# Other places in SBUF for the tile pools of a two-layer encoder kernel

## The chip, the cores and the metric

The kernel runs on one core of one Trainium2 chip. The metric is device time in microseconds of one execution of the whole program: the median of three runs before the change is 2350.79 us (2350.09 to 2352.40). The profile is of one more execution, which took 2351.57 us; from its first to its last instruction it spans 2349.8 us.

## The reference

Two encoder layers on one sequence of 512 tokens, width 1024, in float32, then a final RMSNorm. Cut to what matters:

```python
for l in range(2):
    xn = rmsnorm(x, norm1_g[l])
    h = xn @ w_in[l]                                  # split into the inputs of four mixers
    ys = [gdn_mixer, diff_mixer, swa_mixer, mlstm_mixer]   # each (512 tokens, 512 wide)
    branch = einsum('bsnw,nwd->bsnd', stack(ys), w_branch[l])
    gate = sigmoid(einsum('bsd,dne->bsne', xn, w_gate[l]))
    x = x + sum(gate * branch, axis=2) @ w_out[l]
    xn = rmsnorm(x, norm2_g[l])
    x = x + square(relu(xn @ w_mlp1[l])) @ w_mlp2[l]
return rmsnorm(x, final_norm_g)
```

## The kernel before, in words

Every dense product is computed with operands split into two parts, a high one of type float32r and a low one that holds what is left (`xh` and `xl`, `wh` and `wl`, `hh` and `hl`, `mh` and `ml`), as three matmuls that add up in one PSUM bank: high by high, high by low, low by high. A stream of dense work (projections, gates, merges, MLP) fills the time between the steps of the four mixers, which are written as generators; in the MLP, from the output projection on, the dense stream is alone.

There are three forms of dense work, and the text calls them by their lines.

- L392 to L394 (`run_a`): the activations are the stationary operand (128x128, loaded by LDWEIGHTS) and the weights, 256 columns, move. It does the input projections that are wanted token by token (stationary `xh`, `xl`), the output projection `wo` (stationary `mh`, `ml`) and the second MLP product `m2` (stationary `hh`, `hl`). Line 718 to 720 do the last slice of `m2` in the same order of matmuls, with weights kept in `twh` and `twl`.
- L406 to L408 (`run_b`) and L435 to L437 (`run_b2`): the weights are stationary and 512 columns of activations move.
- L832 to L834: the first MLP product `m1`, a fast scheme of seven products for two by two blocks; weights stationary, 256 columns of activations (`xh`, `xl`, or sums of them, `xsh`, `xsl`) move.

The order of the three matmuls in `run_a`, for one 128-token block `tt` and one 128-row slice `k4`:

```python
th, tl = xh[kt][:, blk(tt)], xl[kt][:, blk(tt)]
mm(o, th, wh[:, k4, :], start=(kt == 0 and tt % 2 == 0), stop=False)     # L392
mm(o, th, wl[:, k4, :], start=False, stop=False)                         # L393
mm(o, tl, wh[:, k4, :], start=False, stop=(kt == kts - 1 and tt % 2 == 1))   # L394
```

Tiles come from six pools in SBUF. A pool takes a stretch of every partition when it is opened, and the stretches follow each other in the order of the lines that open the pools.

```python
def A(dt=F32, s="t", w=S):              # pool ar: 26 buffers
    return ar.tile([P, 516], dt, tag="ar", name=nm(s))[:, :w]
def B(dt=F32, s="b", w=2048):           # pool bg: 13 buffers
    return bg.tile([P, 2080], dt, tag="bg", name=nm(s))[:, :w]
```

`bg` holds the large activation tiles, 2080 values or 8320 bytes a partition: `x`, `xh`, `xl`, `hh`, `hl`, `mh`, `ml`, `twh`, `twl`, the raw weights `wq` of `m1`, and what the mixers keep. `wp` holds the weights of the other dense work, 4096 bytes a partition: two buffers of raw weights (`wr`, filled by DMA), three of `wh`, three of `wl`. `ar` holds 26 tiles of 2064 bytes, placed 2080 apart, for everything of 512 columns, `xsh` and `xsl` among it. `sp` holds columns of a few values, `cp` the constants, `lp` what one layer keeps. A pool hands its buffers out in turn as they come free, so `hh` and `hl` stand in other `bg` buffers each time.

The bytes of a partition that each pool has, in the program before and in the changed one (the first 16512 bytes are taken by other things in both):

| pool | before | changed |
|---|---|---|
| cp | 16512 to 27424 | 211520 to 222432 |
| lp | 27424 to 31392 | 222432 to 226400 |
| wp | 31392 to 64160 | 124672 to 157440 |
| sp | 64160 to 66720 | 226400 to 228960 |
| ar | 66720 to 120800 | 157440 to 211520 |
| bg | 120800 to 228960 | 16512 to 124672 |

Buffer number i of `bg` begins at 120800 + 8320 i before and at 16512 + 8320 i in the changed program. Inside the tiles, the slices that `run_a` reads begin at multiples of 512 bytes.

Of the kernel before, what the change touches and what calls it, by code (L numbers as in the profile page):

```python
# [30 lines left out]
NAR = 26  # L31
NBG = 13
# [81 lines left out]
def encoder(ctx: ExitStack, tc: tile.TileContext, a: dict, out: bass.AP, dbg: dict = None):  # L114
    nc = tc.nc
    dbg = dbg or {}
    pe, dve, act, pool = nc.tensor, nc.vector, nc.scalar, nc.gpsimd
    mm = pe.matmul
    cp = ctx.enter_context(tc.tile_pool(name="cp", bufs=1))
    lp = ctx.enter_context(tc.tile_pool(name="lp", bufs=1))  # L120
    wp = ctx.enter_context(tc.tile_pool(name="wp", bufs=3))
    sp = ctx.enter_context(tc.tile_pool(name="sp", bufs=8))
    ar = ctx.enter_context(tc.tile_pool(name="ar", bufs=NAR))
    bg = ctx.enter_context(tc.tile_pool(name="bg", bufs=NBG))
    dr = ctx.enter_context(tc.tile_pool(name="dr", bufs=1, space=bass.MemoryType.DRAM))
    pd = ctx.enter_context(tc.tile_pool(name="pd", bufs=4, space=bass.MemoryType.PSUM))
    pm = ctx.enter_context(tc.tile_pool(name="pm", bufs=4, space=bass.MemoryType.PSUM))
# [1623 lines left out]
```

## Time and profile before

| | |
|---|---|
| median of three runs | 2350.79 us |
| profiled execution | 2351.57 us |
| its span, first to last instruction | 2349.8 us |
| PE (TensorE matmul) busy | 2285.3 us, 97% |
| PEld (weight load) busy | 2083.2 us, 89% |
| DVE, ACT, POOL busy | 1582.2, 1187.5, 747.6 us |
| mean granted TensorE clock | 0.996 of full speed |
| DMA | 200.72 MB, the hardware queue's packets fill 27.5% of 16 engines' time |

PE is what is busy nearly always. Its matmuls are pipelined: one takes some 280 ns from start to end, while the next starts after less than half of that. So the time that a matmul costs is read from start to start: a stretch of time divided by the matmuls that it starts.

### The profile page before, as it was taken

The page shows a single profiled execution, that of the slowest core. Times are in us where ns is not written, and L with a number is a line of the kernel's source. Part 1 is how long each engine was busy: PE and PEld are TensorE (multiplying, and loading weights), DVE is VectorE, ACT ScalarE, POOL GpSimd, SP SyncE. Part 2 cuts the span into 40 slices and gives each one's busy share as a digit, 9 for nine tenths or more (in the row PEclk, how much of TensorE's full clock was granted, in tenths as well). Part 3 has the DMA queues.
Part 4 walks back from the last instruction along what each step waited for, and adds up shares of the span by engine and source line. Part 5 has one row for each costly group of instructions (what it writes and reads, how often), then busy time and mean ns, then how long its engine had stood idle before and what let it go on. Part 6 is the DMA issues. An engine that isn't in the chain of part 4 may idle for free. (4 is left out here: it accounts for less than half of the span.)

```text
span 2349.8 us, 43335 instructions
## 1 busy us (share of the span) xinstructions
PE 2285.3 (97%) x16992; PEld 2083.2 (89%) x16992; DVE 1582.2 (67%) x2988; ACT 1187.5 (51%) x2777; POOL 747.6 (32%) x806
## 2 busy tenths in 40 slices
PE   7999999999999999999999999999999999999998
PEld 6879987989888989999987799879898889899998
DVE  5774547685786477677767745587767854867775
ACT  4565444654665264344445654365546643534443
POOL 1135552132232134343200555412313310434341
PEclk9999999999999999999999999999999999999999
DMA  6322131222122523333323112321221234233322
GB/s 149 99 46 64 55 95 57 60 88 80 51 71 74 160 71 122 95 109 108 111 74 90 55 55 64 91 63 52 93 82 55 72 106 131 90 97 109 99 82 90
DMA packets 234779, 200.72 MB, mean 85 GB/s; under 512 B 31696, under 2 KB 223824, under 8 KB 234576
## 3 DMA queue, kind: packets, MB, share of 16 engines
q1 hardware_dynamic: 231408, 192.75, 27.5%
q10 hardware_dynamic: 2304, 4.20, 0.5%
q8 instruction: 133, 2.18, 0.4%
q0 software_dynamic: 864, 1.02, 0.2%
q14 instruction: 70, 0.57, 0.1%
HBM read 190.04 MB, written 8.39 MB: 84 GB/s over the span
## 5 line engine op out<-in xcount | busy, mean ns | idle before, releaser
L293 DVE TENSOR_TENSOR wl<-wr,wh 128x512 fp32r<-128x512 f32 x540 | 400.4, 762 | 183.4 <-ACT wh L292 176.1
L292 ACT CAST wh<-wr 128x512 fp32r<-128x512 f32 x540 | 317.0, 621 | 219.0 <-PE pd L436 59.2
L392 PE MATMUL pd<-wh,xh 128*128 128x256 f32 x960 | 279.4, 291 | 0.0
L393 PE MATMUL pd<-wl,xh 128*128 128x256 f32 x960 | 269.8, 281 | 0.0
L394 PE MATMUL pd<-wh,xl 128*128 128x256 f32 x960 | 269.4, 281 | 0.0
L394 PE MATMUL pd<-wh,hl 128*128 128x256 f32 x896 | 248.2, 277 | 0.0
L392 PE MATMUL pd<-wh,hh 128*128 128x256 f32 x896 | 248.0, 277 | 0.0
L393 PE MATMUL pd<-wl,hh 128*128 128x256 f32 x896 | 248.0, 277 | 0.0
L292 ACT CAST wh<-wq 128x512 fp32r<-128x512 f32 x196 | 115.3, 619 | 220.4 <-PE pd L394 94.0
L435 PE MATMUL pd<-xh,wh 128*128 128x512 f32 (+1 forms) x544 | 217.7, 401 | 0.5 <-ACT xh L222 0.5
L436 PE MATMUL pd<-xl,wh 128*128 128x512 f32 (+1 forms) x544 | 209.0, 384 | 1.8 <-DVE xl L223 1.6
L437 PE MATMUL pd<-xh,wl 128*128 128x512 f32 (+1 forms) x544 | 208.8, 384 | 0.0
L293 DVE TENSOR_TENSOR wl<-wq,wh 128x512 fp32r<-128x512 f32 x196 | 181.9, 962 | 13.4 <-ACT wh L292 13.3
L393 PEld LDWEIGHTS pd<-wl,xh 128*128 128x128 f32 x960 | 181.9, 189 | 1.4
L392 PEld LDWEIGHTS pd<-wh,xh 128*128 128x128 f32 x960 | 181.5, 189 | 1.4
L394 PEld LDWEIGHTS pd<-wh,xl 128*128 128x128 f32 x960 | 181.3, 189 | 0.2
L809 POOL TENSOR_TENSOR wq<-wq,wq 128x512 f32<-128x512 f32 x84 | 124.4, 1488 | 163.1 <-DVE wl L293 153.7
L393 PEld LDWEIGHTS pd<-wl,hh 128*128 128x128 f32 x896 | 168.2, 188 | 0.0
L394 PEld LDWEIGHTS pd<-wh,hl 128*128 128x128 f32 x896 | 168.2, 188 | 0.0
L392 PEld LDWEIGHTS pd<-wh,hh 128*128 128x128 f32 x896 | 168.1, 188 | 0.0
L677 DVE TENSOR_TENSOR x<-pd,x 128x512 f32<-128x512 f32 x124 | 85.1, 689 | 101.4 <-PE pd L394 101.4
L1011 POOL TENSOR_TENSOR r<-r,r 128x512 f32<-128x512 f32 (+1 forms) x28 | 35.5, 1266 | 325.8 <-DVE r L1010 185.9
(394 smaller groups left out, 6656.9 us busy)
## 6 DMA issues: line engine op xcount, KB each, us to landing
wr<-in_w_in SPq DMA_DIRECT2D x92, 512.0 KB
wr<-in_w_mlp SPq DMA_DIRECT2D x72, 512.0 KB
wr<-in_w_gate SPq DMA_DIRECT2D x64, 512.0 KB
wq<-in_w_mlp SPq DMA_DIRECT2D x56, 512.0 KB
wr<-in_w_branch SPq DMA_DIRECT2D x32, 512.0 KB
wr<-in_w_out SPq DMA_DIRECT2D x16, 512.0 KB
x<-in_x SPq DMA_DIRECT2D x16, 256.0 KB
gsd<-gs ACTq DMA_DIRECT2D x16, 256.0 KB
```

What stands on the lines that cost most here:

```text
L292: act.copy(wh[:, k:k + n], raw[:, k:k + n])
L293: dve.tensor_tensor(wl[:, k:k + n], raw[:, k:k + n], f(wh[:, k:k + n]), op=ALU.subtract)
L392: mm(o, th, wh[:, k4, :], start=(kt == 0 and tt % 2 == 0), stop=False)
L393: mm(o, th, wl[:, k4, :], start=False, stop=False)
L394: mm(o, tl, wh[:, k4, :], start=False, stop=(kt == kts - 1 and tt % 2 == 1))
L435: mm(o, w1_, xh[kt][:, sl], start=(kt == 0 and hi_ == 0), stop=False)
L436: mm(o, w1_, xl[kt][:, sl], start=False, stop=False)
L437: mm(o, w2_, xh[kt][:, sl], start=False, stop=last)
L677: dve.tensor_tensor(d, bank.rearrange("p (t c) -> p t c", t=2), d, op=ALU.add)
L809: pool.tensor_tensor(d[:, k:k + 2], x[:, k:k + 2], y[:, k:k + 2], op=op)
L1011: pool.tensor_tensor(v(t1), v(t1), v(t2), op=ALU.add)
```

## The change

The lines that open the pools are put in another order: `bg`, `wp`, `ar`, `cp`, `lp`, `sp` in place of `cp`, `lp`, `wp`, `sp`, `ar`, `bg`. Sizes, counts of buffers, tags and all instructions stay. On every engine the instructions of the two programs stand in the same order, row for row, with the same waits and the same buffer numbers; only the byte addresses of the operands in SBUF differ.

```diff
     mm = pe.matmul
+    bg = ctx.enter_context(tc.tile_pool(name="bg", bufs=NBG))
+    wp = ctx.enter_context(tc.tile_pool(name="wp", bufs=3))
+    ar = ctx.enter_context(tc.tile_pool(name="ar", bufs=NAR))
     cp = ctx.enter_context(tc.tile_pool(name="cp", bufs=1))
     lp = ctx.enter_context(tc.tile_pool(name="lp", bufs=1))
-    wp = ctx.enter_context(tc.tile_pool(name="wp", bufs=3))
     sp = ctx.enter_context(tc.tile_pool(name="sp", bufs=8))
-    ar = ctx.enter_context(tc.tile_pool(name="ar", bufs=NAR))
-    bg = ctx.enter_context(tc.tile_pool(name="bg", bufs=NBG))
     dr = ctx.enter_context(tc.tile_pool(name="dr", bufs=1, space=bass.MemoryType.DRAM))
```

In bytes modulo 256, `wp` buffers begin at 160 before and at 0 in the changed program. `bg` buffers begin at 224 (even numbers) and 96 (odd numbers) before, at 128 (even) and 0 (odd) in the changed one. The `ar` tiles take all eight multiples of 32 in both.

The buffer numbers in `bg`, the same in both programs, of the high and low stationary tiles (`hh` and `hl`, or `mh` and `ml`, of which `wo` uses two pairs):

| stretch | layer 0 | layer 1 |
|---|---|---|
| `wo` | 3 and 0, 5 and 2 | 11 and 5, 3 and 12 |
| `m2`, seven in order of time | 0 and 5, 2 and 9, 3 and 0, 10 and 2, 6 and 3, 5 and 10, 9 and 6 | 5 and 3, 12 and 4, 11 and 5, 7 and 12, 10 and 11, 3 and 7, 4 and 10 |
| last slice of `m2` (L718 to L720), with `twh` in 10 and 11, `twl` in 1 and 3 (layer 0); `twh` in 2 and 7, `twl` in 9 and 11 (layer 1) | 0 and 5 | 5 and 3 |

## Rows read from the trace of the kernel before

**Rows 1.** From the page: span, busy time of each engine with its share of the span and its instructions, and the granted TensorE clock in 40 slices of the span (tenths, 9 is 90% or more).
```profile
span 2349.8 us, 43335 instructions
PE 2285.3 (97%) x16992; PEld 2083.2 (89%) x16992; DVE 1582.2 (67%) x2988; ACT 1187.5 (51%) x2777; POOL 747.6 (32%) x806
...
PEclk9999999999999999999999999999999999999999
```

**Rows 2.** Groups of instructions by line and shape, dense matmuls of PE: line, engine, operation, output and inputs, shape, count | busy us in total, mean ns of one from start to end | idle before. Each line's two neighbours, for the other two of its three matmuls, have the same counts.
```profile
L392 PE MATMUL pd<-wh,xh 128*128 128x256 f32 x960 | 279.4, 291 | 0.0
...
L392 PE MATMUL pd<-wh,hh 128*128 128x256 f32 x896 | 248.0, 277 | 0.0
...
L435 PE MATMUL pd<-xh,wh 128*128 128x512 f32 x480 | 198.7, 414 | 0.0
...
L832 PE MATMUL pm<-xsh,wh 128*128 128x256 f32 x448 | 126.1, 282 | 0.0
...
L406 PE MATMUL pd<-xh,wh 128*128 128x512 f32 x304 | 121.3, 399 | 0.0
...
L435 PE MATMUL pd<-yh,wh 128*128 128x512 f32 x256 | 104.8, 410 | 0.0
...
L832 PE MATMUL pm<-xh,wh 128*128 128x256 f32 x336 | 95.3, 283 | 0.0
...
L392 PE MATMUL pd<-wh,mh 128*128 128x256 f32 x192 | 53.3, 278 | 0.0
L718 PE MATMUL pd<-twh,hh 128*128 128x256 f32 x128 | 36.2, 283 | 0.0
```

**Rows 3.** PE in the stretches in which L392 to L394 do `wo` (the 32.70 and the 34.10 us one, 288 matmuls each) and `m2` (192 matmuls each; seven stretches a layer, layer 0 up to 1160 us): the stretch in us from the span's start, its length, PE busy (instructions, those still running at the left edge counted too), granted clock, DMA share, GB/s. The last row sums all sixteen.
```profile
791.37:824.07 32.70, 32.70 (x290) 1.00 0.36 109
888.57:910.37 21.80, 21.80 (x195) 1.00 0.33 97
930.17:951.97 21.80, 21.80 (x194) 1.00 0.28 90
...
1947.17:1981.27 34.10, 34.10 (x289) 1.00 0.32 101
2045.87:2068.47 22.60, 22.60 (x195) 1.00 0.30 94
2088.27:2110.07 21.80, 21.80 (x195) 1.00 0.28 92
2129.87:2152.47 22.60, 22.60 (x194) 1.00 0.29 89
2172.37:2194.17 21.80, 21.80 (x195) 1.00 0.29 93
2213.97:2235.77 21.80, 21.80 (x195) 1.00 0.30 92
2255.57:2278.17 22.60, 22.60 (x194) 1.00 0.35 113
2298.07:2319.87 21.80, 21.80 (x195) 1.00 0.45 138
sum 374.30, PE 374.30; mean PE 23.39
```

**Rows 4.** The same view of four other stretches: two of input projections (L392 to L394 on `xh` and `xl`, 46 and 44 starts), two of the seven products of `m1` (L832 to L834, 168 starts each).
```profile
554.80:560.00 5.20, 5.20 (x49) 1.00 0.05 8
567.30:572.60 5.30, 5.30 (x47) 1.00 0.19 44
910.37:930.17 19.80, 19.80 (x171) 1.00 0.37 117
2068.47:2088.27 19.80, 19.80 (x170) 1.00 0.37 113
```

**Rows 5.** PE in order of time, the last slice of `m2` (L718 to L720): start us, length us, engine, line, output and inputs. Layer 0: its first row and the instruction that follows its first 96 matmuls. Layer 1: its first row and the one that starts 118 matmuls later.
```profile
1160.01 0.28 PE L718 MATMUL pd<-twh,hh 128*128 128x256 f32 x1
...
1171.33 1.04 PE L487 MATMUL pm<-c_ident,nj 128*128 128x128 f32 x8
...
2319.83 0.28 PE L718 MATMUL pd<-twh,hh 128*128 128x256 f32 x1
...
2333.90 0.28 PE L719 MATMUL pd<-twl,hh 128*128 128x256 f32 x1
```

**Rows 6.** PE on 512 columns. First two unbroken stretches of L406 to L408 and L435 to L437 (310 and 309 starts), as in rows 3; then four matmuls of a mixer whose two operands both stand in `bg`, in order of time.
```profile
38.19:110.20 72.01, 72.01 (x312) 1.00 0.38 100
1198.71:1269.89 71.18, 71.18 (x311) 1.00 0.35 98
...
1681.67 0.39 PE L1535 MATMUL pm<-bkh,bq 128*128 128x512 f32 x1
1681.90 0.39 PE L1536 MATMUL pm<-bkl,bq 128*128 128x512 f32 x1
1682.13 0.39 PE L1535 MATMUL pm<-bkh,bq 128*128 128x512 f32 x1
1682.36 0.40 PE L1536 MATMUL pm<-bkl,bq 128*128 128x512 f32 x1
1682.60 0.60 PE L1550 MATMUL pm<-c_ident,p 128*128 128x128 f32 x4
```

**Rows 7.** All engines in the stage from 150 to 830 us (columns as in rows 3, one busy time for each engine), one piece of the chain that ended last (start us, length us, what), the hardware DMA queue (packets, MB, share of 16 engines' time), and the same elementwise operations on tiles of `ar` in two uses each (as in rows 2).
```profile
150.00:830.00 680.00, 665.18 (x4933) 592.24 (x4931) 441.03 (x988) 353.92 (x931) 220.57 (x240) 0.99 0.26 78
...
1993.77 4.14 DMA wq<-in_w_mlp
...
q1 hardware_dynamic: 231408, 192.75, 27.5%
...
L1499 ACT ACTIVATE W<-R,mb 128x128 f32<-128x128 f32 x96 | 32.1, 392 | 0.0
L1499 ACT ACTIVATE W<-Rm,mb 128x128 f32<-128x128 f32 x64 | 23.2, 393 | 0.0
```

## The prediction

> **What bounds the kernel now.** I read the head of the page first. PE is busy for 2285.3 of 2349.8 us, 97%, the next engine for 67%, and the granted clock is in the top tenth in all 40 slices [rows 1]. So no wait sets the time; what sets it is how quickly PE starts one matmul after another.
>
> The change moves no instruction and no wait. Only addresses differ, so the time moves only where a duration depends on an address. Elementwise work shows no such place: one ACT operation reads different `ar` tiles at 392 and 393 ns [rows 7].
>
> PE does. The groups by line and shape hint at it: a 128x256 matmul of L392 lasts 277 ns on `hh`, 278 on `mh`, 291 on `xh` [rows 2]. The windows say it plainly. Each of the fourteen `m2` stretches starts 192 matmuls; those shown take either 21.80 or 22.60 us, with PE busy throughout and the clock at 1.00 [rows 3]. That is 21.80/192 = 113.5 ns from start to start, or 22.60/192 = 117.7 ns. The DMA share does not sort them: 0.28 with 21.80, 0.29 with 22.60, and 0.33 and 0.45 with 21.80 again. Nor does weight loading or waiting, the program text of the stretches being the same. What sorts them is the buffer table of the change: the stretches at 22.60 have `hh` and `hl` in 5 and 3, 11 and 5, 3 and 7, odd numbers both; every shown one at 21.80 has an even number in the pair. (The sum of all sixteen, 374.30, leaves 307.5 us for the fourteen, which is eleven at 21.80 and three at 22.60, so the rows left out are fast too, and their pairs have even numbers.) Likewise `wo`: layer 0, with pairs 3,0 and 5,2, takes 32.70/288 = 113.5 ns, layer 1, with 11,5 and 3,12, takes 34.10/288 = 118.4 ns.
>
> Before the change `wp` begins at 160 modulo 256, an even `bg` buffer at 224 (distance 64) and an odd one at 96 (distance 192). So the reading is that a 256-column matmul has two rates, about 113.3 and 118.5 ns, and that the distance between the stationary and the moving operand helps to choose. It does not choose alone. Pair 3,12 has an even buffer and lies in the slow stretch, and the input projections, on the same `xh` tiles all along, take 5.20/46 = 113.0 ns in one stretch and 5.30/44 = 120.5 ns in another [rows 4]. So I take it for a preference, with some memory of the matmuls before.
>
> **What the changed addresses bring.** `wp` now begins at 0, even `bg` buffers at 128, odd ones at 0: the distances become 128 and 0. The whole forecast hangs on the rate at these two. One place already has them: the last slice of `m2`, where weights and activations both stand in `bg`, so that two buffers differ by 0 or 128 in either program. Layer 0 goes from 1160.01 to 1171.33 with 96 matmuls, 117.9 ns each; layer 1 from 2319.83 to 2333.90 with 118, 119.2 ns each [rows 5]. Both follow a fast `m2` stretch, so they were not slow by inheritance, and the pair of layer 0 is 0 and 5, with an even number in it. The rate that I carry over is the mean, 118.5 ns.
>
> Term one, `wo` and `m2` in `run_a`: 2x288 + 14x192 = 3264 matmuls, now 374.30 us together [rows 3], 114.7 ns each. At 118.5 they take 386.8 us: **+12.5 us**. Bounds: all at 113.3, 369.8 us, gives -4.5; all at 119.2, 389.1 us, gives +14.8.
>
> Term two, the input projections of L392 to L394: 3x960 = 2880 matmuls [rows 2], whose two clean stretches average 116.7 ns [rows 4]. At 118.5: 2880 x 1.8 ns = **+5 us**. Bounds: if all were at 113.0 now, +16; if all were at 118.5 now, 0; if all fall to 113.3, -10.
>
> Term three, `m1`: 3x(448 + 336) = 2352 matmuls [rows 2], fourteen stretches of 168, of which both shown take 19.80/168 = 117.9 ns [rows 4]. Those of the 448 group move `ar` tiles, which meet the weights at all eight distances before and after. All stand near the slow rate already: **0**. Bounds: all at 113.3 gives -10.8, all at 119.2 gives +3.1.
>
> Term four, 512 columns (L406 to L408, L435 to L437), 3x(480 + 304 + 256) = 3120 matmuls [rows 2]. Two long stretches take 72.01/310 = 232.3 and 71.18/309 = 230.4 ns, and a mixer's pair with both operands in `bg`, at distances of 0 or 128, starts every 230 ns, at 1681.67, 1681.90, 1682.13 and 1682.36 [rows 6]. That is the rate of today: **0**. No row shows 512 columns at either extreme; by twice the 256-column rates, 226.6 and 238.4 ns against a mean of 231.4, the bounds are -15 and +22.
>
> Everything else. From 150 to 830 us PE is busy 665.18 of 680.00 us [rows 7]; the idle 2% can swallow 2% of what PE gains or loses there, mostly term two: under 0.2 us. DVE, ACT and POOL have the same work on the same kind of tiles, and lie under a PE that is 97% busy: **0**, and up to the same percent of slack if they did slow. DMA: the queue fills 27.5% of its engines' time, and one 4.14 us transfer of `wq` stands on the chain of what ended last [rows 7]. The same packets go to other addresses: 0, at most some tenths of that one transfer, +-1.
>
> The sum is 12.5 + 5 + 0 + 0 = +17.5 us on the profiled 2351.57, or 2369.1. The profiled execution lies 0.8 us above the median of 2350.79, so against that median the forecast is **2368 us**.
>
> **The rivals.** First, faster. The distances 128 and 0 may suit the fast rate when the moving operand stands in `wp`, and the slow tail may come from something else, for instance both operands in one pool or its strict alternation of four weight tiles. Then the terms go toward their lower bounds, -4.5 - 10 - 10.8 - 15 = -40 at most; half of that, since no group of today is all fast, is -20: 2331 us. For it: apart from `wo` and `m2`, the groups of today lie in the middle or near the slow rate, so that three terms have more to win than to lose. Against it: the only rows at these distances, from both layers, are slow. It decides as soon as more of the `wo` and `m2` matmuls run fast than today's eleven stretches of 192 and one of 288: 2400 of 3264, 74%.
>
> Second, no change: the rates are reshuffled by history and not by distance, other stretches become fast and slow, and the sum over some 11,000 matmuls stays, 2351 +- 5 us. For it: the projections take both rates on the same tiles [rows 4]. Against it: all three slow `m2` stretches have odd pairs, and no fast one has. [...]
>
> Third, slower still: 512 columns follow as well. Terms one and two at 119.2 ns give 14.8 + 7.2, `m1` +3.1, the 512-column matmuls +22 at their bound: +47, 2398 us; with half of the last, 2387.
>
> **How the numbers follow.** A measurement of this kernel can tell about 0.2%, 4.7 us. The forecast, between 2358 (just over half of term one alone) and 2382 (the first three terms at 119.2 ns, 14.8 + 7.2 + 3.1 = +25, and a quarter of the 512-column bound), has a chance of 0.57; no change 0.17; faster 0.20, since two tails of some hundred matmuls carry the whole forecast; slower still 0.06. Faster is then 0.20, same 0.17, slower 0.57 + 0.06 = 0.63. The range goes from 2334, which takes in no change and most of the faster case's milder half, to 2386; outside lie about half of faster and of slower still, 0.13, and a little of each other case.
>
> **What would show it.** If right, the fourteen `m2` stretches of the changed kernel all read about 22.7 us and the even and odd pairs no longer differ, both `wo` stretches read about 34.1, the mean of L392 on `hh` and `mh` rises from 277 and 278 toward the 283 ns of L718 [rows 2], the tail reads the same 117.9 and 119.2, and DVE, ACT, POOL and the clock stay. If those stretches stand at 21.80 throughout, the carry-over from the tail was the wrong step; if they mix as today, distance does not choose. A moved mean of 512 columns beyond 230 to 232 ns would break term four, and with its many matmuls the sum.

## The result

The changed kernel takes 2367.63 us (2366.23 to 2371.96, four runs) against 2350.97 for the kernel before beside it: a ratio of 1.0073, 95% interval 1.0056 to 1.0091. The forecast was 2368, slower. The first lines of the page of the changed kernel:

```profile
span 2366.5 us, 43335 instructions
PE 2304.6 (97%) x16992; PEld 2106.6 (89%) x16992; DVE 1581.5 (67%) x2988; ACT 1187.5 (50%) x2777; POOL 747.1 (32%) x806
...
PEclk9999999999999999999999999999999999999999
```

Beside [rows 1]: the span has grown by 16.7 us and PE is busy for 19.3 us more, while DVE, ACT and POOL have not changed by a microsecond each and the granted clock has stayed at 0.996 of full speed. The added time is PE's. (PE's first matmul starts 8.16 us after the first instruction, 8.87 before, so PE from there on takes some 17.4 us more.) Here are the stretches of `wo` and `m2`, the same view as [rows 3] (stretch, length, PE busy, granted clock, DMA share, GB/s; the last row sums all sixteen):

```profile
790.79:825.10 34.31, 34.31 (x290) 1.00 0.33 103
889.60:912.32 22.72, 22.72 (x195) 1.00 0.30 93
...
974.91:997.78 22.87, 22.87 (x195) 1.00 0.27 86
...
1957.98:1992.41 34.43, 34.43 (x290) 1.00 0.32 99
2056.87:2079.89 23.02, 23.02 (x195) 1.00 0.29 92
2099.80:2122.58 22.78, 22.78 (x195) 1.00 0.27 87
...
sum 388.46, PE 388.46; mean PE 24.28
```

No stretch is at 21.80 any more; the sixteen take 388.46 us in place of 374.30. The other stretches of [rows 4 to 6], found in the new trace by the same matmuls (46, 45, 168, 168, 310, 309, 96 and 118 starts):

```profile
554.30:559.78 5.48, 5.48 (x49) 1.00 0.11 18
567.30:572.66 5.36, 5.36 (x47) 1.00 0.21 58
912.32:932.26 19.94, 19.94 (x171) 1.00 0.36 114
2079.89:2099.80 19.91, 19.91 (x171) 1.00 0.36 113
38.37:109.01 70.64, 70.64 (x311) 1.00 0.37 99
1207.58:1278.30 70.72, 70.72 (x311) 1.00 0.35 98
1168.75:1180.09 11.34, 11.34 (x99) 1.00 0.64 141
2336.49:2350.55 14.06, 14.06 (x121) 1.00 0.10 38
```

Projections that took 5.20 us take 5.48; those that were slow already are as slow (45 starts, 119.1 ns each). `m1` rises from 19.80 to 19.94 and 19.91. The 512-column stretches have become faster, 72.01 to 70.64 and 71.18 to 70.72, or 227.9 and 228.9 ns a start. The last slice of `m2`, whose distances the change does not touch, stays: 11.32 and 14.07 before [rows 5], 11.34 and 14.06 now. The groups by line and shape say it once more, the same view as [rows 2] and, for the last, [rows 7] (L392 on `mh` rises from 278 to 282 as well):

```profile
L392 PE MATMUL pd<-wh,xh 128*128 128x256 f32 x960 | 282.8, 295 | 0.0
...
L392 PE MATMUL pd<-wh,hh 128*128 128x256 f32 x896 | 252.6, 282 | 0.0
...
L718 PE MATMUL pd<-twh,hh 128*128 128x256 f32 x128 | 36.2, 283 | 0.0
...
L1499 ACT ACTIVATE W<-R,mb 128x128 f32<-128x128 f32 x96 | 32.1, 391 | 0.0
```

Since both programs hold the same matmuls in the same order, each start-to-start time can be set against its twin, and the differences added up by line:

| matmuls | difference, us | ns a start where nothing interrupts |
|---|---|---|
| L392 to L394 on `hh`, `hl` | +12.2 | 114.4 to 119.0 |
| L392 to L394 on `mh`, `ml` | +2.0 | 115.9 to 119.3 |
| L392 to L394 on `xh`, `xl` | +6.6 | 116.1 to 118.9 |
| L832 to L834 (`m1`) | +1.2 | 118.0 to 118.6 |
| 512 columns, L406 to L408 and L435 to L437 | -4.7 | 231.7 to 230.0 |
| two small groups: L435 to L437 on 256 columns, and the last slice of `wo` (L741 to L743) | +0.6 | 117.2 to 119.3 |
| last slice of `m2` | 0.0 | 118.6 to 118.6 |
| all other | -0.5 | |
| sum | +17.4 | |

### The profile page after: what moved, and what is told of

It is laid out like the page before. It is cut to its first block, busy times and chain, and to the rows that moved or that the text cites. A ratio compares the mean times of both kernels' runs of the same rounds, so it can differ in the third digit from the quotient of the medians.

```text
span 2366.5 us, 43335 instructions
## 1 busy us (share of the span) xinstructions
PE 2304.6 (97%) x16992; PEld 2106.6 (89%) x16992; DVE 1581.5 (67%) x2988; ACT 1187.5 (50%) x2777; POOL 747.1 (32%) x806
## 5 line engine op out<-in xcount | busy, mean ns | idle before, releaser
L392 PE MATMUL pd<-wh,xh 128*128 128x256 f32 x960 | 282.8, 295 | 0.0
L394 PE MATMUL pd<-wh,xl 128*128 128x256 f32 x960 | 272.6, 284 | 0.0
L392 PE MATMUL pd<-wh,hh 128*128 128x256 f32 x896 | 252.6, 282 | 0.0
L394 PE MATMUL pd<-wh,hl 128*128 128x256 f32 x896 | 252.5, 282 | 0.0
L292 ACT CAST wh<-wq 128x512 fp32r<-128x512 f32 x196 | 115.3, 619 | 234.4 <-PE pd L394 103.7
L435 PE MATMUL pd<-xh,wh 128*128 128x512 f32 (+1 forms) x544 | 217.1, 400 | 0.5 <-ACT xh L222 0.5
L437 PE MATMUL pd<-xh,wl 128*128 128x512 f32 (+1 forms) x544 | 208.2, 383 | 0.0
L392 PEld LDWEIGHTS pd<-wh,xh 128*128 128x128 f32 x960 | 182.6, 190 | 1.3
L394 PEld LDWEIGHTS pd<-wh,xl 128*128 128x128 f32 x960 | 182.4, 190 | 0.3
L392 PEld LDWEIGHTS pd<-wh,hh 128*128 128x128 f32 x896 | 169.8, 189 | 0.0
L394 PEld LDWEIGHTS pd<-wh,hl 128*128 128x128 f32 x896 | 169.6, 189 | 0.0
```

The source lines that it names most:

```text
L292: act.copy(wh[:, k:k + n], raw[:, k:k + n])
L435: mm(o, w1_, xh[kt][:, sl], start=(kt == 0 and hi_ == 0), stop=False)
L437: mm(o, w2_, xh[kt][:, sl], start=False, stop=last)
```

## The experiments

All programs below hold the same instructions in the same order as the kernel before; only addresses in SBUF differ. Each has one trace. The table lists each with the distance from `wp` to `bg` modulo 256 that it gives, its time (median) and ratio to the kernel before in the same set of runs, the sum of the sixteen stretches, and how many of the fourteen `m2` stretches (at most 21.83 us) and of the two of `wo` (at most 32.9) are fast in its trace.

| kernel | distance | us | ratio, 95% interval | sixteen stretches | fast `m2`, `wo` |
|---|---|---|---|---|---|
| before | 64 even, 192 odd | | 1 | 374.26 | 11, 1 |
| changed | 128 even, 0 odd | 2367.63 | 1.0073 (1.0056 to 1.0091) | 388.46 | 0, 0 |
| e1 | 64, 192 in the new homes | 2352.69 | 1.0001 (0.9991 to 1.0010) | 374.25 | 11, 1 |
| e2 | 128, 0 in the old homes | 2367.41 | 1.0067 (1.0050 to 1.0084) | 388.46 | 0, 0 |
| e3 | 192, 64 | 2354.06 | 1.0012 (1.0002 to 1.0022) | 378.65 | 5, 2 |
| e4 | 64, 192, all 32 bytes further | 2352.46 | 1.0002 (0.9993 to 1.0012) | 374.27 | 11, 1 |
| e5 | 64 all | 2343.80 | 0.9959 (0.9947 to 0.9972) | 373.55 | 13, 0 |
| e6 | 192 all | 2366.15 | 1.0061 (1.0046 to 1.0076) | 384.42 | 0, 0 |
| e7 | 96, 224 | 2369.64 | 1.0075 (1.0055 to 1.0095) | 385.62 | 0, 0 |
| e8 | 160, 32 | 2371.56 | 1.0083 (1.0062 to 1.0104) | 389.18 | 0, 0 |
| e9 | `hh`, `mh` 192, others 64 | 2359.58 | 1.0036 (1.0024 to 1.0049) | 386.37 | 0, 1 |
| e10 | as e9 in the new homes | 2362.34 | 1.0046 (1.0032 to 1.0060) | 385.34 | 1, 1 |
| e11 | `hh`, `mh`, `xl` 192, others 64 | 2345.76 | 0.9975 (0.9966 to 0.9985) | 373.20 | 14, 0 |
| e12 | `hh`, `ml`, `xl` 192, others 64 | 2344.50 | 0.9966 (0.9953 to 0.9978) | 370.14 | 14, 2 |

### Is it the distance or the home?

Four kernels take the two apart. The first (e1) keeps the new homes and restores the distances:

```diff
     bg = ctx.enter_context(tc.tile_pool(name="bg", bufs=NBG))
+    ctx.enter_context(tc.tile_pool(name="pad", bufs=1)).tile([P, 16], F32, tag="pad", name="pad")
     wp = ctx.enter_context(tc.tile_pool(name="wp", bufs=3))
     ar = ctx.enter_context(tc.tile_pool(name="ar", bufs=NAR))
```

> The changed kernel with 64 unused bytes between bg and wp. wp, ar and the small pools move up by 64 bytes, so that wp begins at 64 modulo 256 and the distances from wp to bg are again 64 (even buffers) and 192 (odd), as before the change, while every pool keeps its new home. Theory (distance modulo 256 chooses the rate of PE): wo and m2 return to eleven fast m2 stretches of 21.80 us and three slow ones of 22.60 us with the pairs 5 and 3, 11 and 5, 3 and 7, and the input projections return with them; time 2351 us, within 4 us. Rival (the home itself, far up or down in SBUF, or the order of the pools): all stretches stay slow at about 22.8 us, time 2367 us, within 3.

Measured: 2352.69 us, ratio 1.0001. The stretches of its trace:

```profile
885.18:907.00 21.82, 21.82 (x194) 1.00 0.30 97
...
2043.99:2066.61 22.62, 22.62 (x194) 1.00 0.29 94
sum 374.25, PE 374.25; mean PE 23.39
```

That is the kernel before [rows 3], stretch by stretch to 0.02 us, although every tile lies elsewhere by tens of thousands of bytes. The second kernel (e2) does the reverse: the old order of pools, and the same pad of 64 bytes ahead of `bg`, so that only `bg` moves.

```diff
     ar = ctx.enter_context(tc.tile_pool(name="ar", bufs=NAR))
+    ctx.enter_context(tc.tile_pool(name="pad", bufs=1)).tile([P, 16], F32, tag="pad", name="pad")
     bg = ctx.enter_context(tc.tile_pool(name="bg", bufs=NBG))
```

> The kernel before with 64 unused bytes between ar and bg: bg alone moves, by 64 bytes, to distances 128 (even) and 0 (odd) from wp, the distances of the changed kernel. Nothing else moves. Theory (distance): all fourteen m2 stretches slow at 22.6 to 22.9 us and both wo stretches at about 34.1, wo and m2 together +14, the projections +6, 512 columns -4; time 2366 us, within 4 us. Rival (home): 2351 us, within 3, with eleven fast m2 stretches.

Measured: 2367.41 us, ratio 1.0067, in its trace:

```profile
...
888.75:911.46 22.71, 22.71 (x194) 1.00 0.30 93
...
2056.02:2079.04 23.02, 23.02 (x195) 1.00 0.30 92
...
sum 388.46, PE 388.46; mean PE 24.28
```

These are the stretches and the sum of the changed kernel. The difference by line is also its own: L392 to L394 on `hh` +12.2, on `mh` +2.0, on `xh` +7.0, `m1` +1.0, L406 to L408 and L435 to L437 together -5.3 (in the changed kernel -4.3), the last slice of `m2` 0.0. So 64 bytes ahead of `bg` bring the whole loss, and 64 bytes ahead of `wp` take it back. The third kernel (e4) moves everything by 32 bytes, which makes the starts of `wp` and `bg` multiples of 64, as they are in the changed kernel.

```diff
+    ctx.enter_context(tc.tile_pool(name="pad", bufs=1)).tile([P, 8], F32, tag="pad", name="pad")
     cp = ctx.enter_context(tc.tile_pool(name="cp", bufs=1))
```

> The kernel before with 32 unused bytes ahead of the first pool: every address in SBUF grows by 32, so that wp and bg begin at multiples of 64, as in the changed kernel, while all distances stay. Theory (distance): no change, 2351 us, within 3, the same stretches fast and slow. Rival (what counts is whether an operand begins at a multiple of 64 bytes): the changed kernel's 2367 us, within 4.

Measured: 2352.46 us, ratio 1.0002, and the same eleven stretches fast with a sum of 374.27. Whether operands begin at multiples of 64 bytes or 32 bytes beside them makes no difference here; what counts is how two operands stand to each other. That the homes of the pools, or their order, cost anything is excluded to 0.1% by the interval of the first kernel.

### Which distances are good?

The fourth kernel (e3) exchanges even and odd, with 128 bytes ahead of `bg`:

```diff
+    ctx.enter_context(tc.tile_pool(name="pad", bufs=1)).tile([P, 32], F32, tag="pad", name="pad")
     bg = ctx.enter_context(tc.tile_pool(name="bg", bufs=NBG))
```

> The kernel before with 128 unused bytes between ar and bg: the distances are 192 (even buffers) and 64 (odd), today's values with even and odd exchanged. Theory (a stretch is fast when at least one of hh and hl stands at distance 64): the m2 stretches with two even buffers become the slow ones, that is the fourth of layer 0 (10 and 2) and the second and the seventh of layer 1 (12 and 4, 4 and 10), at 22.60 us, and the other eleven, with 5 and 3, 11 and 5, 3 and 7 among them, take 21.80; time 2351 us, within 5 us. Rival (the stretch, its place in the program or the buffers' own places decide): the slow three are those of today.

Measured: 2354.06 us, ratio 1.0012. The time is near, but the expected pattern is wrong:

```profile
884.73:907.55 22.82, 22.82 (x195) 1.00 0.28 93
...
970.00:991.79 21.79, 21.79 (x195) 1.00 0.29 92
1011.50:1034.11 22.61, 22.61 (x195) 1.00 0.27 89
...
1951.42:1984.29 32.87, 32.87 (x289) 1.00 0.34 106
2048.62:2071.24 22.62, 22.62 (x195) 1.00 0.30 94
```

The stretch of 10 and 2 (at 1011.50), now both at 192, is slow as expected. But 5 and 3 (at 2048.62), now both at 64, is slow too, and 0 and 5 (at 884.73), with one of them at 64, is slow at 22.82, while 3 and 0 (at 970.00) is fast. Five `m2` stretches are fast, not eleven. So "one of the two at 64 is enough" falls. The rival (the places in the program decide) falls as well, since `wo` of layer 1 has become fast. That stretch changes its rate within itself. It works by turns of 48 matmuls with two pairs, one at 64 and 64, one with the high part at 64 and the low part at 192. The first three turns (first pair, second pair, first pair again):

```profile
1951.42:1957.07 5.65, 5.65 (x50) 1.00 0.30 98
1957.07:1962.53 5.46, 5.46 (x50) 1.00 0.48 153
1962.53:1967.97 5.44, 5.44 (x50) 1.00 0.30 99
```

The first pair starts at 117.7 ns, the second comes to the fast rate, and then the first, in the same buffers, starts every 113.3 ns. So at one and the same distances a pair can have either rate.

Two kernels (e5 and e6) then bring all of `bg` to one distance. A tile of `bg` has 2080 columns and nearly all uses want 2048, so a tile can begin 32 columns later at no cost of memory:

```diff
     def B(dt=F32, s="b", w=2048):
-        return bg.tile([P, 2080], dt, tag="bg", name=nm(s))[:, :w]
+        t = bg.tile([P, 2080], dt, tag="bg", name=nm(s)); o = 32 * (cnt[0] in ODD); return t[:, o:o + w]
```

`ODD` stands for a set of numbers written out in the kernel: the tiles that come to lie in odd buffers. The second of the two has the even ones there.

> The kernel before, with the 2048 columns that are used of a bg tile of 2080 begun 32 columns (128 bytes) later in the odd buffers, so that every bg tile stands at distance 64 from wp. Same instructions in the same order. Theory A (64 is a good distance, 192 a bad one that a pair survives when its other half stands at 64): all fourteen m2 stretches at 21.78 us and both wo at 32.67, -3.9 us; projections from 116.1 to about 114.5 ns a start, -4.6 us; 512 columns +2.5; time 2345 us, within 5. Theory B (64 and 192 are alike; each allows a fast and a slow state, and what runs just before a stretch decides in which one it stays): fast and slow stretches still stand side by side, time 2351 us, within 6.

> The same with the even buffers shifted instead, so that every bg tile stands at distance 192 from wp. Theory A: no stretch is fast, all m2 stretches at 22.6 us and wo at 33.9, +11 us, projections +5, 512 columns -2; time 2365 us, within 4. Theory B: like the other, a mixture, 2351 us, within 6.

Measured: all at 64, 2343.80 us, ratio 0.9959, faster than the kernel before; all at 192, 2366.15 us, ratio 1.0061. Both were forecast within 1.2 us by theory A. Of the stretches with all at 64:

```profile
786.94:820.86 33.92, 33.92 (x290) 1.00 0.34 106
884.20:906.82 22.62, 22.62 (x195) 1.00 0.31 95
...
1943.69:1977.61 33.92, 33.92 (x290) 1.00 0.33 103
2043.13:2064.90 21.77, 21.77 (x195) 1.00 0.27 88
...
sum 373.55, PE 373.55; mean PE 23.35
```

Thirteen of fourteen `m2` stretches are fast, but the first is not, and both of `wo` are slow (33.92 us, 117.8 ns a start) at the very distance at which `m2` is fast. The gain was expected from `wo` and `m2` (-3.9 us) and projections (-4.6); by line it is -1.8 on `hh`, +1.1 on `mh`, -0.5 on `xh`, -4.4 on L406 to L408 and L435 to L437, and -1.1 on `m1`, -5.6 with the rest, of the 5.7 us by which its span is shorter. So the total was right for another reason than the one given. With all at 192 no stretch is fast; every `m2` stretch takes 22.61 or 22.62:

```profile
890.01:912.62 22.61, 22.61 (x194) 1.00 0.29 93
```

Here too the total came by other parts than forecast: `wo` and `m2` +10.2 (forecast +11), projections +2.8 (+5), and the 512-column matmuls +4.5 where -2 was forecast. Two more kernels (e7 and e8) try distances between, with 32 and with 96 bytes ahead of `bg`:

```diff
+    ctx.enter_context(tc.tile_pool(name="pad", bufs=1)).tile([P, 8], F32, tag="pad", name="pad")
     bg = ctx.enter_context(tc.tile_pool(name="bg", bufs=NBG))
```

```diff
+    ctx.enter_context(tc.tile_pool(name="pad", bufs=1)).tile([P, 24], F32, tag="pad", name="pad")
     bg = ctx.enter_context(tc.tile_pool(name="bg", bufs=NBG))
```

> The kernel before with 32 unused bytes between ar and bg: distances 96 (even) and 224 (odd), which no run has shown. If the fast state exists only at odd multiples of 64, all stretches are slow as at 0 and 128, time 2367 us, within 5; if it exists at every distance other than multiples of 128, stretches are fast as today or more often, 2345 to 2352 us.

> The kernel before with 96 unused bytes between ar and bg: distances 160 (even) and 32 (odd). As for the run with 32 bytes: 2367 us, within 5, if only odd multiples of 64 allow the fast state, 2345 to 2352 us if only multiples of 128 forbid it.

Measured: 2369.64 and 2371.56 us, ratios 1.0075 and 1.0083, not one fast stretch in either. With the changed kernel and its twin in the old homes that makes 64 stretches at distances 0, 32, 96, 128, 160 and 224, none fast, as the first alternative said.

### What else decides at 64 and 192?

If a stretch can be fast or slow at one distance (`m2` 22.62 and 21.78 us in e5), something else must choose, and what runs ahead of it may be that. The pairs of the kernel before suggested that a stationary pair whose high and low part stand at different distances comes to the fast rate by itself: all eight `m2` stretches with such a pair took 21.76 to 21.82 us, although the last twelve starts of `m1` ahead of each came every 117.8 ns. The edit is the line of the two kernels with one distance, with other sets (e9, e10 and e11); the second of the three also has the new order of pools with 64 bytes between `bg` and `wp`.

```diff
-        return bg.tile([P, 2080], dt, tag="bg", name=nm(s))[:, :w]
+        t = bg.tile([P, 2080], dt, tag="bg", name=nm(s)); o = 32 * (cnt[0] in SHIFTED); return t[:, o:o + w]
```

`SHIFTED` stands for the numbers of `hh` and `mh` in even buffers and of all other tiles in odd ones, and in the third kernel of `hh`, `mh` and `xl` in even buffers and of all other tiles in odd ones.

> As the run with every bg tile at distance 64, but hh and mh, the high parts that wo and m2 hold stationary, stand at 192, and their low parts at 64; all other bg tiles at 64. In the kernel before, the pairs with the high part at 192 and the low part at 64 are 3 and 0 (wo and m2 of layer 0), 5 and 10, 9 and 6, 7 and 12: all fast, after 2 to 5 starts. With all at 64 both wo stretches (33.92 us) and one m2 stretch (22.61) came out slow. Theory (a pair that alternates between 64 and 192 leaves the slow state by itself, a pair at one distance keeps the state that it enters with): all fourteen m2 stretches at 21.77 and both wo at 32.67; 3 us less than with all at 64, 2341 us, within 4. Rival (what comes before a stretch decides whatever the pair): wo stays at 33.9, 2344 us.

> The same distances in the changed kernel's homes (64 unused bytes between bg and wp, hh and mh at 192, every other bg tile at 64). If distance is all: the same stretches to 0.05 us each and the same time as that run in the old homes, within 3 us. If the home has a price of its own, the difference is that price.

> As the run with hh and mh at 192, and xl at 192 as well, so that the pair xh, xl of the input projections alternates too (64 and 192). Theory: the projections leave the slow state and come from about 115.3 to 113.6 ns a start, -4.9 us; the third of the 512-column matmuls that moves xl goes from 229.7 to 233 ns, +2.5 us; in sum 2 us less than that run. Rival (the projections are interrupted by the mixers too often to hold any state): no gain, 512 columns +2.5, 2 us more.

Measured: 2359.58 us (ratio 1.0036), 2362.34 us (1.0046) and 2345.76 us (0.9975). The first is a clear miss: 2341 was expected. Its stretches of `m2` are all slow, and those of the third all fast, although `hh` and `hl` stand alike in both and the stationary pair of `m2` has the same two distances. The second `m2` stretch, first of the kernel with `xl` at 64 (e9), then with `xl` at 192 (e11):

```profile
...
927.10:949.93 22.83, 22.83 (x195) 1.00 0.26 86
...
```

```profile
...
927.31:949.08 21.77, 21.77 (x195) 1.00 0.27 89
...
```

`xl` takes no part in `m2`. It is moved by `m1`, right ahead of each `m2` stretch. The two timelines of PE at the start of the second stretch (start us, length, line, operands), first with `xl` at 64, then at 192:

```profile
926.99 0.28 PE L834 MATMUL pm<-xh,wl 128*128 128x256 f32 x1
927.10 0.28 PE L392 MATMUL pd<-wh,hh 128*128 128x256 f32 x1
...
928.05 0.28 PE L394 MATMUL pd<-wh,hl 128*128 128x256 f32 x1
928.17 0.28 PE L392 MATMUL pd<-wh,hh 128*128 128x256 f32 x1
```

```profile
927.19 0.28 PE L834 MATMUL pm<-xh,wl 128*128 128x256 f32 x1
927.31 0.28 PE L392 MATMUL pd<-wh,hh 128*128 128x256 f32 x1
...
927.54 0.28 PE L394 MATMUL pd<-wh,hl 128*128 128x256 f32 x1
...
928.22 0.28 PE L394 MATMUL pd<-wh,hl 128*128 128x256 f32 x1
```

In the slow one nine starts cover 1.07 us, 119 ns each, and so it goes on to the end; in the fast one the last six of these starts, from 927.54 to 928.22, take 0.68 us, 113 ns each, and it stays there too. So between these two kernels the matmuls ahead decide which rate the stretch takes (22.83 or 21.77 us), and the pair keeps it for a hundred and eighty starts. What they hand on is not their own rate: the last 24 starts of `m1` ahead of this stretch take 2.83 us, 117.9 ns each, in both kernels, first with `xl` at 64, then at 192:

```profile
924.27:927.10 2.83, 2.83 (x26) 1.00 0.20 68
```

```profile
924.48:927.31 2.83, 2.83 (x26) 1.00 0.24 75
```

In all ten traces at distances of 64 and 192 the last twelve starts ahead of an `m2` stretch average 117.6 to 118.2 ns, whichever rate follows. What is handed on instead, the traces do not show.

The theory that an alternating pair heals itself falls for a high part at 192 and a low part at 64 (fourteen stretches at 22.82 or 22.83 us in e9); the rival (what comes before decides) holds for `m2`. It does not tell which history is good: that was found by trying. The third kernel was forecast 2 us below the first and lies 13.8 us below it, nearly all of it in `m2`, for which no change was forecast. The gain forecast for the projections did not come: they take 115.3 ns an uninterrupted start with `xl` at 192, 115.4 with it at 64, 1.7 us less in all where 4.9 were expected; and the 512-column matmuls that move `xl` stayed at 230 ns where 233 was expected.

The same distances in the new homes give the same stretches but one (the first `m2` of layer 1, 21.77 in place of 22.82), and times whose intervals overlap. A price of the home does not show, but the one stretch does: the distances between `wp` and `bg` alone do not fix every history. Ahead of that stretch, and of no other `m2` stretch of this trace, `m1` waits for a `wl` that DVE writes; from one start to the next 445 ns pass, 17 starts before the stretch:

```profile
2045.81 0.28 PE L833 MATMUL pm<-xl,wh 128*128 128x256 f32 x1
2046.26 0.39 PE L834 MATMUL pm<-xh,wl 128*128 128x256 f32 x1 [0.17 <-DVE wl L293]
```

The one slow `m2` stretch of e5 has such a pause at the same place (461 ns), and it alone of the fourteen. But ahead of one stretch each of e1, e4, e9 and e11 a pause of 453 to 471 ns made no difference to what followed. So the pause is a lead and not a cause that is shown; with one trace of each kernel it is also not known how often such a stretch turns from one execution to the next.

The last kernel (e12) is the third of these with `mh` and `ml` exchanged in the set.

> As the run with hh, mh and xl at 192, but with mh and ml exchanged: mh at 64, ml at 192 (hh and xl at 192, every other bg tile at 64). wo was slow in all runs of this series but one of its stretches, with mh and ml both at 64 and with mh at 192. In the kernel before, pairs with the high part at 64 and the low part at 192 became fast after 9 starts (0 and 5, 2 and 9, 6 and 3, 10 and 11). Theory (this order leaves the slow state wherever it comes from): both wo stretches at about 32.9 us instead of 34.24, m2 as before this exchange (21.77 in all fourteen), 2.7 us less than that run, 2343 us, within 4, the fastest of all. Rival (what runs just before wo keeps it slow whatever the pair): wo 33.9 to 34.3, 2346 us.

Measured: 2344.50 us, ratio 0.9966. Both stretches of `wo` and all of `m2` are fast:

```profile
786.80:819.49 32.69, 32.69 (x289) 1.00 0.35 108
...
1943.30:1975.98 32.68, 32.68 (x289) 1.00 0.35 107
...
sum 370.14, PE 370.14; mean PE 23.13
```

This agrees with the theory in its numbers (2343 expected, both `wo` stretches named). The other traces bear it out. The `m2` stretches of the ten traces at 64 and 192, counted by the distances of their pair:

| high part, low part | fast `m2` stretches |
|---|---|
| 64, 192 | 16 of 16 (before, e1, e3, e4) |
| 64, 64 | 22 of 26 |
| 192, 64 | 42 of 72 |
| 192, 192 | 0 of 26 |

The order 64, 192 was fast each time, the pair at 192, 192 never, and the two others took either rate. That the first order comes to the fast rate from every history is still more than these traces can show, since the histories tried are few. The kernel beats both kernels, by 0.34% the one before, and with the kernel that has all at 64 (ratio 0.9959) it is the best found; their intervals overlap.

## Why the prediction was right

**What bounds the kernel.** Right. PE's start-to-start rate carries the whole difference, +17.4 us; the engines beside it did not move by 1 us, and the tail, with unchanged distances, took the same time to 0.02 us.

**That distance chooses the rate.** Right for this change, and shown: 64 bytes restore the old time in the new homes (e1, ratio 1.0001) and give the new time in the old homes, where moving one pool by 64 bytes and nothing else cost 0.67% (e2). What makes the starts later, no run shows.

**The rate carried over from the last slice of `m2`.** Right in kind. 118.5 ns was taken; `wo` and `m2` came out at 119.0, the projections at 118.9. Term one was +12.5 and measured +14.2, term two +5 and +6.6. Part of the second miss is a slip of mine in reading [rows 4]: the slow stretch of projections, matched matmul by matmul, has 45 starts in 5.35 us, 119.0 ns, not 44 in 5.30; with 119.0 the mean of the two would have been 116.0, the rate of the whole trace is 116.1, and the term +7. The stretches are at 22.7 to 23.0 and 34.3 to 34.4, a little over the 22.7 and 34.1 that were named. And the even and odd pairs still differ, which the prediction had ruled out: `m2` takes 22.7 us with an even high and an odd low buffer, 22.8 with two even ones, 22.9 with odd and even, 23.0 with two odd ones, and the same to 0.02 us in e2.

**`m1` at zero.** 118.0 became 118.6 ns, +1.2 us, inside its bounds.

**512 columns at zero.** This term was mis-sized: -4.7 us. The mixer's pair at 230 ns was read as the rate at the new distances; the dense stretches went to 227.9 and 228.9. Where `bg` moves and `wp` is stationary the two groups of buffers moved apart: over all uninterrupted starts, activations in odd buffers (weights minus activations 64 before, 0 now) went from 232.2 to 229.0 ns, 1620 starts, and those in even ones (192 before, 128 now) from 230.3 to 231.1, 958 starts. A bound of -15 to +22 had been left for it.

**The sum.** The forecast of +17.5 meets +17.4 of the traces because the terms that were too small (3.3 us in the first two, 1.2 in the third) and the one that was missed (-4.7) nearly cancel. The forecast's range would have held without that; its closeness is luck.

**The memory of the matmuls before.** It was named as a reserve, and it is half of the truth: at distances 64 and 192 the same pair was fast or slow by what ran ahead (21.77 us in e11, 22.83 in e9). It did not hurt the forecast, since at the new distances no stretch was fast, none of 32 in two traces, whatever came before.

**What stays open.** Why 64, alone or together with 192, and none of the other distances tried, lets a stretch be fast; which history leads to which rate, and what it hands on; and why `wo` and `m2` differ with all at 64. The pads also move `bg` against `ar` and the constants, which other engines read and write; that the operands of the matmul are what counts is argued from the steady rates, and no run separates the two. Distances between multiples of 32 bytes were not tried.

## What to carry to other kernels

Where matmuls follow each other without a gap, read the time from start to start of each stretch, not the mean duration of one: here two stretches with the same text took 21.77 and 22.61 us, both repeated to 0.02 us in three kernels (before, e1, e4), and that pointed to the places of their operands. Where such a place may matter, move one pool by a pad of 64 bytes before moving pools about (here the pad alone gave the ratio 1.0067 in the old homes, e2, and 1.0001 in the new, e1), and look at the distance between the stationary and the moving operand, not at the place of either; in this kernel it was taken modulo 256, and 89 of 160 stretches were fast at 64 and 192, none of 64 at the others. Even a buffer's stride can put neighbours into different classes, as the 8320 bytes of `bg` did with 64 and 192, so a tile that begins some columns later is a cheap way to choose the class of each tile: 32 columns brought ratios from 0.9959 (e5) to 1.0061 (e6). What it gains has to be measured as a whole, because what ran ahead of a stretch had a part in its rate here (22.83 us in e9, 21.77 in e11).

## What the runs showed of the hardware

- In `m2` a 128x256 float32r matmul started every 113.3 to 113.6 ns (21.76 to 21.82 us for 192) or every 117.3 to 121 ns (22.52 to 23.23 us), at the same granted clock of 1.00. In all 196 `m2` stretches of the fourteen traces the rate after the first 24 starts stayed to the end, within 0.7 ns.
- The choice mostly repeated: the kernel before, e1 and e4, whose pools lie elsewhere but at the same distances, show the same sixteen times to 0.02 us (sums 374.26, 374.25 and 374.27), and so do the changed kernel and e2 (388.46 both). Of e9 and e10 one stretch of sixteen differs, 22.82 and 21.77 us.
- Of 64 stretches at distances of 0, 32, 96, 128, 160 and 224 bytes modulo 256 none was fast; of 160 at 64 and 192, 89 were, and none of those whose parts all stood at 192.
- The one elementwise operation compared shows nothing of it: ACT (L1499) took 392 and 391 ns before and after.
